# Hybrid decoder block on one core: heads 0 and 1 join the first seven-product column group, now 768 columns wide in six PSUM banks

## The chip, the cores and the metric

The kernel runs on one core of one Trainium2 chip. The metric is the device time of one execution in microseconds (us); the median of three runs of the kernel before is 1599.9 us. The engines are PE (TensorE, matmuls), ACT (ScalarE), DVE (VectorE), POOL (GpSimd) and SP, whose queue issues most transfers.

## The reference

The block normalizes `x` (1024 tokens by 2048), multiplies it by one wide input matrix, runs three groups of heads on the columns of the product, gates them, and adds an output projection:

```
h = rmsnorm(x, ln_g);  proj = h @ w_in          # 1024x2048 by 2048x7184
(g_u, g_v, g_z, d_q, d_k, d_v, d_z, d_a, d_b, c_q, c_z) = split(proj)
out_a = gmlp_spatial_gating(g_u, g_v, ...) * silu(g_z)
q, k, v = split(causal_conv_silu(concat(d_q, d_k, d_v), conv_w))   # 8 heads of 128 each
out_b = rmsnorm(gated_delta_rule(l2norm(q), l2norm(k), v, g, beta)) * silu(d_z)
out_c = softmax((c_q @ mk^T)) @ mv * silu(c_z)  # mk, mv from 256 memory rows
y = rmsnorm(x + concat(out_a, out_b, out_c) @ w_out)
```

Only the columns of q, k and v of the delta heads (group B), heads 0 to 3, and what feeds them are touched by the change.

## The kernel before, in words

**Products.** Every float32 operand is split into a rounded high part (ACT copies it to the float32r type) and a low part (DVE subtracts), by `split_to` (L445); a product of two blocks is then three matmuls, high by high, high by low, low by high (`triple`). A matmul has a 128 x 128 stationary block and 512 moving columns (tokens here).

**Stages.** First the keys and values of the memory rows are made (16 blocks of the contraction, `kvmark`), while `x`'s first 512 tokens are normalized, transposed on PE and split into the resident tiles `ahq`, `alq` (16 blocks of 128 contraction rows; `ahi[k]`, `alo[k]`). Then comes the stage that the change rewrites:

- Heads 0 and 1 have their q and k columns (four blocks of 128 columns) projected directly, for each half of the tokens: `project_first` (L889) for the first column block, `project` (L876) for the others, called from `conv` (L913). One column block and one token half is 16 contraction blocks times three matmuls. `project_first` runs its sixteen blocks twice with 256 tokens each, so that it can begin before the last 256 tokens are ready. After the first half of the tokens, `x`'s second half is normalized and transposed (`prep1`, L773), kept in plain form in tiles of the rings `ut`, `kT`, `qT`, `kd`, `ai`, `vs`, `gt`, and split once more into `ahq`, `alq` for the second half's projections. Banks: `main_bank` (L420) gives acc0 and acc1 to the projections in turn, `tpb` (L424) acc2 and acc3 to the transposes of `prep1` and to the decays.
- `decay_mm`, `decay_rows`, `decays` (L802 to L817) make the decay and beta columns of all heads, for each half.
- `left_sums` (L753) makes four sums and differences of the left factor's quarters and stores them to DRAM (`s_all`, in the profile `sa`); `whole` (L747) stores the plain left factor (`h0d`).
- Then the columns go two groups of 512 at a time through a scheme of seven products in place of eight: the left factor (tokens by contraction) is cut into 2 x 2, the two column groups and the two halves of the contraction make the right factor's 2 x 2, and `seven` (L1338) runs seven products of 512 tokens by 1024 contraction rows by 512 columns. `ORDER` is 2, 1, 6, 5, 3, 7, 4: products 2 and 1 make the first output quarter, product 1's sum stays in PSUM and 6, 7 and 4 accumulate on it. Four banks hold a product (`wide`, L1311), one for each block of 128 columns. For each product, right blocks are loaded from `w_in`, combined on DVE, and split; left blocks are loaded from `h0d`, `hTd` or `sa` and split. `blocks(5)` (L1510) does so with the q and k columns of heads 2 and 3 as one group (512 columns) and v of heads 0 to 3 as the other.

**Fronts.** `front` (L1174) does, for two heads and one token half, the convolution (`conv`), the transposes and small products of `qk` (L950), stores q, k, kd and ai for later (`late`), and feeds the 32 x 32 blocks to `inverse` (L1007). Fronts of heads 0 and 1 read their q and k from PSUM, those of the other heads from DRAM (`pd`). `backs` (L1495) later runs the recurrent scan of each pair of heads. After `blocks(5)` follow `blocks(0)` to `blocks(4)` with four banks each, and the output projection.

**Order.** Operations are not issued in program order: `Plan` records them all with a cost, a class (`rank`) and their dependencies, simulates the engines, and issues each engine's instructions in the simulated order. Main matmuls have class 9; whatever is ready with a lower class goes ahead of them. A tile that takes another tile's place (`heir`) waits for all users of the old one. All instructions carry the line of `issue` (L300) in the profile, so groups are told apart by tile.

Of the kernel before, what the change touches and what calls it, by code (L numbers as in the profile page):

```python
# [303 lines left out]
def kernel(  # L304
# [95 lines left out]
    for r in (wraw, whi, wlo):  # L400
        r.bufs = [b[:, i * HT : (i + 1) * HT] for b in r.bufs for i in range(2)]
    whi.bufs.append(C([P, HT], "whi4", F32R))
    wlo.bufs.append(C([P, HT], "wlo4", F32R))
# [14 lines left out]
    turn = {"acc": 0, "tp": 0, "dn": 0}  # L418

    def main_bank():  # L420
        turn["acc"] += 1
        return acc[turn["acc"] % 2]

    def tpb():  # L424
        turn["tp"] += 1
        return acc[2 + turn["tp"] % 2]
# [21 lines left out]

    def raw_piece(src, cls=4):
        raw = wraw()  # L450
        v = raw if src.ndim == 2 else raw.rearrange("p (k c) -> p k c", k=src.shape[1])
        with rank(cls):
            Q.dma_start(v, src)
        return raw

    def split_piece(raw):
        hi, lo = whi(), wlo()
        with rank(2):
            split_to(hi, lo, raw, V)
        return hi, lo  # L460

    marks = []
# [48 lines left out]
    def load_x(tt, tag, after=(None,) * 4):  # L511
        x_rows[tt] = row_tiles(tag)
        for c in range(4):
            with behind(after[c] or R.gate):
                Q.dma_start(x_rows[tt][c], x[tt * P : (tt + 1) * P, c * HT : (c + 1) * HT])
# [45 lines left out]
    def prep(tt, put, bank):  # L561

        xq = x_rows[tt]
        r = row_scale(xq)
        for q in range(NQ):
            V.scalar_tensor_tensor(xq[q], xq[q], r, gb[q], op0=ALU.mult, op1=ALU.mult)
            tp = bank()
            for k in range(4):
                PE.transpose(tp[:, k * P : (k + 1) * P], xq[q][:, k * P : (k + 1) * P], ident)
            put(q, tok(tp))  # L570

    def keep_rows(dst, q, tt, tp):
        t = ring["tn"]()
        S.copy(t, tp.rearrange("p t c -> p (t c)"))
        Q.dma_start(dst[4 * q : 4 * q + 4, :, tt * P : (tt + 1) * P].rearrange("k p n -> p k n"), tok(t))
# [24 lines left out]
    for k in range(KT):  # L600
# [49 lines left out]
        if k == 13:  # L650
            load_x(3, "qT", (kvmark[10], kvmark[11], kvmark[11], kvmark[12]))
            with rank(2):
                prep(2, put0(2), spare)
# [6 lines left out]
    for mt in range(2):  # L660
        t = [ring["ai"](F32R) for _ in range(2)]
        S.activation(t[0], va[mt], AF.Copy, scale=rm[mt])
        V.scalar_tensor_tensor(t[1], va[mt], rm[mt], t[0], op0=ALU.mult, op1=ALU.subtract)
        for i in range(2):
            Q.dma_start(
# [3 lines left out]
    with rank(2):  # L669
        prep(3, put0(3), spare)  # L670
    for h in range(NX):
        t = ring["vs"](F32R).rearrange("p (s m) -> p s m", s=2)
        split_to(t[:, 0], t[:, 1], kfs[h], V)
        Q.dma_start(kv_d[0, h], t.bitcast(F32))
# [5 lines left out]
    Q.dma_start(rows[0:96], conv_w.rearrange("k (c p) -> (k c) p", p=P))  # L680
    Q.dma_start(rows[96:100], gmlp_ln_g[0].rearrange("(c p) -> c p", p=P))
    Q.dma_start(rows[100:104], gmlp_ln_b[0].rearrange("(c p) -> c p", p=P))
    Q.dma_start(rows[104:105], dn_norm_g)
# [7 lines left out]
    pt = dnr()  # L691
    PE.transpose(pt[:, 0:105], rows[0:105], ident[0:105, 0:105])
    cw = C([P, 96], "cw")
    V.tensor_scalar(cw, pt[:, 0:96], 0.5, None, op0=ALU.mult)
    col2 = C([P, 9], "col2")
    V.tensor_copy(col2, pt[:, 96:105])

    abf = ring["E"]()[:, 0 : KT * 16].rearrange("p (k c) -> p k c", c=16)
    Q.dma_start(abf, w_in[:, C_AB : C_AB + 16].rearrange("(k p) c -> p k c", p=P))
    abw = C([P, KT * 32 + 96], "abw", F32R)  # L700
    R.users[abw.tensor.name] = []
    V.tensor_scalar(abw[:, KT * 32 :], ident[:, 0:96], 0.0, None, op0=ALU.mult)
    abv = abw[:, 0 : KT * 32].rearrange("p (k c) -> p k c", c=32)
    S.copy(abv[:, :, 0:16], abf)
    V.tensor_tensor(out=abv[:, :, 16:32], in0=abf, in1=abv[:, :, 0:16], op=ALU.subtract)

    halo = C([P, 3 * NH // 2, 3], "halo")
    G.memset(halo, 0.0)
# [22 lines left out]
    pairs = ((C_Q + HT, C_K + HT), (C_DZ + HT, C_DZ), (C_DV + HT, C_V), (C_U, C_Z), (C_CZ, C_CQ), (None, C_DV))  # L731
# [9 lines left out]
    def blk(w, k, c0):  # L741
        if c0 is None:
            both_ = w[k * P : (k + 1) * P, C_Q : C_Q + 2 * DW].rearrange("p (s c) -> p s c", c=DW)
            return both_[:, :, 2 * P : NJ * P]
# [7 lines left out]

    def left_sums(tt, q):  # L753

        def rows_of(d, q):
            return d[4 * q : 4 * q + 4, :, tt * P : (tt + 1) * P].rearrange("k p n -> p k n")

        a, b = spares(), spares()
        c, d = x_rows[NT + tt][q], x_rows[NT + tt][q + 2]
        Q.dma_start(tok(a), rows_of(h0_d, q))  # L760
        Q.dma_start(tok(b), rows_of(h0_d, q + 2))
# [3 lines left out]
        V.tensor_tensor(out=b, in0=b, in1=a, op=ALU.subtract)  # L765
        for i, t in enumerate((d, a, c, b)):
            Q.dma_start(rows_of(s_all[i], q), tok(t))
# [5 lines left out]
    def prep1(i):  # L773
# [6 lines left out]
        prep(NT + i, put, tpb)  # L780
# [21 lines left out]
    def decay_mm(a, k):  # L802
        wk = abw[:, k * 32 : k * 32 + P]
        mm(a, wk, ahi[k], k == 0, False)
        mm(a, wk, alo[k], False, k == KT - 1)

    def decay_rows(a, tt):

        with R.together():
            for q in range(NQ):  # L810
                for j in range(4):
                    k = 4 * q + j
                    PE.matmul(a[j * 32 : (j + 1) * 32, tt * P : (tt + 1) * P],
                              abw[:, k * 32 : (k + 1) * 32].bitcast(F32), tok(x_rows[NT + tt][q])[:, j],
                              start=q == 0, stop=q == NQ - 1)

    def decays(hf, a, bank):  # L817

        NU, M = NT * NH, P if hf else 32
        ab = ring["tn"]()[0:M]  # L820
        with rank(1):
# [7 lines left out]
        with rank(1):  # L829
# [41 lines left out]
    def w_parts(c0, kp):  # L871

        src = w_in[kp * KP * P : (kp + 1) * KP * P, c0 : c0 + P].rearrange("(k p) c -> p k c", p=P)
        return [tok(t) for t in split_piece(raw_piece(src))]

    def project(c0s, order=range(KT // KP)):  # L876

        banks = [main_bank() for _ in c0s]
        for kp in order:
            ws = [w_parts(c0, kp) for c0 in c0s]  # L880
            for kk in range(KP):
                k = kp * KP + kk
                for a, (hi, lo) in zip(banks, ws):
                    triple(a, (hi[:, kk], lo[:, kk]), ahl(k), kp == order[0] and kk == 0, kp == order[-1] and kk == KP - 1)
                if kk == 0:
                    marks.append(R.ops[-3])
        return banks

    def project_first(c0):  # L889

        a, ws = main_bank(), [w_parts(c0, kp) for kp in range(KT // KP)]
        for lo, hi in ((0, NT // 2), (NT // 2, NT)):
            for k in range(KT):
                w = [t[:, k % KP] for t in ws[k // KP]]
                triple(a[:, lo * P : hi * P], w, [t[:, lo:hi] for t in ahl(k)], k == 0, k == KT - 1)
        return a

    def next_job():
        if todo:
            with behind(marks[-1]):  # L900
                todo.pop(0)()

# [7 lines left out]
    def column(which, h):  # L910
        return (C_Q, C_K, C_DV)[which] + h * P

    def conv(which, h, hf, o, a=None):  # L913
# [3 lines left out]
        if which < 2 and h < 2:  # L917
            if a is None:
# [912 lines left out]
```

## Time and profile before

| what | value |
|---|---|
| three runs | 1599.76, 1599.9, 1601.36 us |
| profiled execution: span from the first to the last instruction | 1597.8 us |
| profiled execution's own time | not given apart from the three runs; the median lies 2.1 us above the span |
| DVE busy | 1314.9 us (82%) |
| ACT busy | 1040.0 us (65%) |
| moved by DMA | 428.93 MB, mean 268 GB/s |

The page shows the busy share of each engine over the span, the chain of work that ended last, and groups of like instructions with their mean duration and the idle time ahead of them. Matmuls overlap, so that the distance between the starts of two matmuls, and not the duration of one, is what each costs. In this trace the memory stage ends at about 62.5 us, the direct projections and `blocks(5)` fill the time until about 350 us, and the output projection takes the last 300 us.

### The profile page before, as it was taken

How to read it: one execution, taken by the hardware profiler on the slowest of the kernel's cores; microseconds unless marked ns; L12 is line 12 of the kernel's file. 1: busy time of each engine (PE TensorE's matmuls, PEld its weight loads, DVE VectorE, ACT ScalarE, POOL GpSimd, SP SyncE). 2: the span in 40 equal slices, each digit the busy share in tenths (PEclk: the TensorE clock that was granted, in tenths of full speed). 3: DMA queues.
4: the chain of work that ended last, by engine and by line, in shares of the span. 5: the costliest groups of instructions: out<-in, count | busy, mean ns of one | idle time of the engine just before them, and what ended most of it. 6: DMA issues, size and time to landing. Idle time of an engine off the chain costs nothing.

```text
span 1597.8 us, 26025 instructions
## 1 busy us (share of the span) xinstructions
PE 1582.5 (99%) x8580; PEld 1332.5 (83%) x8580; DVE 1314.9 (82%) x2157; ACT 1040.0 (65%) x2184; POOL 278.6 (17%) x456
## 2 busy tenths in 40 slices
PE   9999999999999999999999999999999999999997
PEld 8878888888888888888888888888888888888886
DVE  6879899869899999998988776867778788778776
ACT  7767648747755788976666667676566874344355
POOL 0101202211411412324342233032000000000001
PEclk9999999999999999999999999999999999999999
DMA  9987997897689868997789875788878879688746
GB/s 340 300 246 206 355 337 229 273 333 249 191 272 339 277 219 295 323 315 242 239 271 341 257 260 178 252 305 279 288 244 260 263 250 335 201 281 279 228 146 241
DMA packets 272744, 428.93 MB, mean 268 GB/s; under 512 B 30633, under 2 KB 97762, under 8 KB 272610
## 3 DMA queue, kind: packets, MB, share of 16 engines
q1 hardware_dynamic: 251138, 371.02, 70.9%
q0 software_dynamic: 20864, 55.20, 10.4%
q8 instruction: 67, 1.10, 0.3%
q10 hardware_dynamic: 608, 1.06, 0.2%
q14 instruction: 67, 0.55, 0.1%
HBM read 339.58 MB, written 87.06 MB: 267 GB/s over the span
## 4 chain that ended last, share of the span: by engine, by line
PE 94%; DMA 2%; ACT 1%; DVE 1%; issue 1%; SPq 0%; POOLq 0%; POOL 0%; ACTq 0%; DVEq 0%
PE acc L300 73%; PE dn L300 22%; DMA qT<-in_x_dram 0%; DMA h0d<-tn 0%; ACT whi L300 0%; DMA wraw<-in_w_in_dram 0%; DMA kvd<-vs 0%; DMA y<-h0d 0%; DMA wraw<-in_w_mem_kv_dram 0%; ACT jk L300 0%; SPq L300 0%; ACT tn L300 0%; DVE wlo L300 0%; ACT ahi L300 0%; DVE kT L300 0%
## 5 line engine op out<-in xcount | busy, mean ns | idle before, releaser
L300 PE MATMUL acc<-ahi,whi 128*128 128x512 f32 (+1 forms) x1488 | 513.4, 392 | 2.3 <-ACT ahi L300 1.1
L300 PE MATMUL acc<-ahi,wlo 128*128 128x512 f32 (+1 forms) x1040 | 404.8, 391 | 0.2 <-DVE wlo L300 0.2
L300 PEld LDWEIGHTS acc<-ahi,whi 128*128 128x128 f32 x1488 | 278.1, 188 | 57.0 <-ACT ahi L300 1.3
L300 PE MATMUL acc<-alo,whi 128*128 128x512 f32 (+1 forms) x592 | 229.2, 387 | 0.0
L300 PEld LDWEIGHTS acc<-ahi,wlo 128*128 128x128 f32 x1040 | 195.5, 188 | 37.2 <-DVE wlo L300 0.6
L300 ACT CAST ahi<-raws 128x1024 fp32r<-128x1024 f32 x148 | 155.4, 1050 | 64.0 <-PE acc L300 27.7
L300 PE MATMUL acc<-ahi,zh 128*128 128x512 f32 x448 | 176.5, 394 | 0.0
L300 PE MATMUL acc<-alo,zh 128*128 128x512 f32 x448 | 176.3, 394 | 0.0
L300 PE MATMUL acc<-ahi,zl 128*128 128x512 f32 x448 | 176.3, 394 | 0.0
L300 ACT CAST whi<-wraw 128x1024 fp32r<-128x1024 f32 (+1 forms) x116 | 108.0, 932 | 94.4 <-PE acc L300 75.6
L300 DVE TENSOR_TENSOR wlo<-wraw,whi 128x1024 fp32r<-128x1024 f32 (+1 forms) x116 | 124.2, 1073 | 38.0 <-ACT whi L300 34.4
L300 PEld LDWEIGHTS acc<-alo,whi 128*128 128x128 f32 x592 | 111.4, 188 | 20.8
L300 POOL TENSOR_TENSOR small<-small,mhalf 128x1 f32<-128x1 f32 x26 | 17.3, 672 | 525.0 <-DVE small L300 525.0
L300 DVE TENSOR_TENSOR alo<-raws,ahi 128x1024 fp32r<-128x1024 f32 x74 | 90.3, 1220 | 19.0 <-ACT ahi L300 18.4
L300 ACT CAST ahi<-y 128x1024 fp32r<-128x1024 f32 x74 | 77.7, 1049 | 40.3 <-PE dn L300 19.2
L300 DVE TENSOR_TENSOR alo<-y,ahi 128x1024 fp32r<-128x1024 f32 x74 | 90.3, 1220 | 16.1 <-ACT ahi L300 15.9
L300 DVE TENSOR_TENSOR ahi<-raws,ahi 128x1024 fp32r<-128x1024 f32 x74 | 90.4, 1222 | 15.1 <-ACT ahi L300 14.5
L300 PEld LDWEIGHTS acc<-alo,zh 128*128 128x128 f32 x448 | 84.2, 188 | 16.3
L300 PEld LDWEIGHTS acc<-ahi,zl 128*128 128x128 f32 x448 | 84.2, 188 | 16.1
L300 PEld LDWEIGHTS acc<-ahi,zh 128*128 128x128 f32 x448 | 84.2, 188 | 16.0
L300 PE MATMUL dn<-whi,ahi 128*128 128x512 f32 x224 | 77.1, 389 | 0.0
L300 PE MATMUL acc<-whi,ahi 128*128 128x512 f32 x216 | 74.9, 392 | 0.0
(464 smaller groups left out, 3451.4 us busy)
## 6 DMA issues: line engine op xcount, KB each, us to landing
wraw<-in_w_in_dram SPq DMA_DIRECT2D x224, 256.0 KB, 4.4
raws<-sa SPq DMA_DIRECT2D x128, 256.0 KB, 4.4
y<-in_w_in_dram SPq DMA_DIRECT2D x96, 256.0 KB, 4.1
y<-sa SPq DMA_DIRECT2D x64, 256.0 KB, 4.2
wraw<-in_w_out_dram SPq DMA_DIRECT2D x64, 256.0 KB, 4.4
raws<-h0d SPq DMA_DIRECT2D x62, 256.0 KB, 5.3
raws<-sd SPq DMA_DIRECT2D x44, 256.0 KB, 2.9
pd<-y SPq DMA_DIRECT2D x40, 256.0 KB, 5.2
```

What stands on the lines that cost most here:

```text
L300: o.fn(*o.args, **o.kw)
```

## The change

The direct projections go. The first pair of column groups becomes 768 wide: one group holds q and k of heads 0 to 2, the other q and k of head 3 and v of heads 0 to 3 (`FIRST_COLS`). A new function runs the seven products with six blocks of 128 columns each, in acc0 to acc3 and dn0, dn1; transposes, decays and fronts share dn2 and dn3 meanwhile. The order of the products is 2, 1, 6, 7, 4, 5, 3. Products 2 and 1 take the left factor from the resident tiles of the first token half, without a load or a split; the second half of the tokens is no longer split into the resident tiles. The first three contraction blocks of product 2 run with 256 tokens at a time.

```diff
-    first = project_first(column(0, 0))
...
-    first = project([column(0, 0), column(1, 0)], (1, 0, 2, 3))
...
-    blocks(5, half_heads, first_values)
...
+    wide6 = acc + dnr.bufs[0:2]
+    FIRST_COLS = (((C_Q, 3 * P), (C_K, 3 * P)), ((C_Q + 3 * P, P), (C_K + 3 * P, P), (C_DV, HT)))
...
+    def first_product(m, take):
+        def left(j, u):
+            if m in (1, 2):
+                k = j + NH * (m == 2)
+                return ahi[k], alo[k]
+            if u == 0:
+                lefts[:] = h_left(m, (j, j + 1))
+            return [x_[:, u * HT : (u + 1) * HT] for x_ in lefts]
...
+        if m == 2:
+            begin = 3
+            ws = [right_first(m, j) for j in range(begin)]
+            for ts in (slice(0, H0), slice(H0, NT)):
+                for j in range(begin):
+                    for t in range(6):
+                        cell(t, j, ws[j], left(j, j % 2), ts)
+        held = []
+        for j in range(begin, NH):
+            a, w = left(j, j % 2), right_first(m, j)
+            if j >= NH - 2:
+                held.append((j, w, a))
+            else:
+                for t in range(6):
+                    cell(t, j, w, a)
...
+        for t in range(6):
+            for h in held:
+                cell(t, *h)
+            take(t, wide6[t])
```

`cell` is one `triple`. The order of the stage is now:

```diff
+    for i in range(NT):
+        prep1(i); decay_rows(strips, i); left_sums(i, 0); left_sums(i, 1)
...
+    for k in (*range(NH, KT), *range(NH)):
+        decay_mm(dnr.bufs[2], k)
...
+    first_product(2, lambda t, a: c11.append((t, a)))
+    ywide = [heir(ahq[2], "y0", "ahi2"), heir(alq[3], "y1w", "alo3"), heir(ahq[3], "y2w", "ahi3")]
...
+    for t, a in c11:
+        keep(yu6[t], a)
...
+    first_product(1, c11_done)
...
+        fronts((0, 0), (1, 0))
+        fronts((2, 0))
...
+    first_product(6, lambda t, a: keep(yz6[t], a))
+    first_product(7, lambda t, a: keep(yu6[t], a))
+    first_product(4, c21_done)
+    first_product(5, closing(1, 1, yu6))
...
+    first_product(3, closing(0, 1, yz6))
...
+        fronts((0, 1), (1, 1))
+        fronts((2, 1))
+        fronts((3, 1), (3, 0))
```

(The first hunk is folded onto one line here.) `fronts` takes any list of heads and halves and reads q and k from DRAM always. The right blocks of product 1 stay in `kept1`, eight tiles of 768 columns (the tile of the spatial weights `wsbt`, a slot of `inv`, `kvraw` and the space of `alq[2]`), and serve product 6 by differences in place (`meet`). `left_sums` no longer loads the plain left factor from DRAM, it adds the resident high and low parts, and stores three of the four sums; the fourth is made when product 3 loads its left blocks (`last_sum`). The weights of the first products have three raw slots (two of `kvraw` and a slot of `inv` that the memory stage holds to its end). The stores of the memory keys and values, their splits, the loads of `x` and the constants get other ranks, and `prep` takes the last two token blocks in the order of quarters 2, 3, 0, 1. The spare fifth bufs of the weight rings become two plain tiles `et`. `blocks(0)` to `blocks(4)`, the scan and the output projection keep their form.

446 lines of the change are left out of this document (237 added, 209 removed).

## Prediction

> **What bounds the kernel now.** I read the head of the page, then the chain of waits, then the busy time by stretches. First the page's span, its busy line, and the chain that ended last by engine:
>
> ```profile
> span 1597.8 us, 26025 instructions
> PE 1582.5 (99%) x8580; PEld 1332.5 (83%) x8580; DVE 1314.9 (82%) x2157; ACT 1040.0 (65%) x2184; POOL 278.6 (17%) x456
> PE 94%; DMA 2%; ACT 1%; DVE 1%; issue 1%; SPq 0%; POOLq 0%; POOL 0%; ACTq 0%; DVEq 0%
> ```
>
> PE is 94% of the chain, and idle for 1597.8 - 1582.5 = 15.3 us. As matmuls overlap, "busy" alone proves little; but if PE is never idle, each matmul that goes is worth the distance between two starts. The stretches of the stage that changes (62.5 to about 350 us) and of what follows show where PE is idle (us of the stretch, then busy time and instructions of PE, PEld, DVE, ACT, POOL, granted clock, DMA share, GB/s):
>
> ```profile
> 62.50:100.00 37.50, 33.78 (x215) 28.95 (x214) 31.62 (x75) 27.64 (x71) 2.80 (x4) 1.00 0.92 265
> 100.00:165.00 65.00, 64.67 (x435) 54.44 (x434) 56.71 (x112) 47.19 (x122) 8.35 (x12) 1.00 0.75 218
> 165.00:229.00 64.00, 63.82 (x303) 52.89 (x302) 57.69 (x113) 35.55 (x70) 10.87 (x21) 1.00 1.07 348
> 229.00:300.00 71.00, 71.00 (x331) 59.25 (x330) 64.71 (x98) 51.53 (x114) 15.82 (x23) 1.00 0.78 249
> 350.00:430.00 80.00, 80.00 (x374) 66.81 (x373) 73.96 (x109) 56.88 (x119) 12.57 (x23) 1.00 0.72 237
> 430.00:500.00 70.00, 70.00 (x315) 58.05 (x314) 63.55 (x115) 34.25 (x51) 14.27 (x25) 1.00 0.86 277
> 510.00:590.00 80.00, 80.00 (x386) 67.11 (x385) 73.60 (x118) 62.31 (x139) 28.05 (x46) 1.00 0.80 265
> 590.00:670.00 80.00, 80.00 (x381) 67.00 (x380) 72.08 (x113) 70.21 (x145) 23.15 (x30) 1.00 0.88 294
> ```
>
> From 62.5 to 165 us PE waits 3.72 + 0.33 = 4.05 us, later hardly at all, even where DMA runs at 348 GB/s and DVE at over 90%. The clock is full throughout. So the stage is bound by the count of matmuls, plus a few starting waits. Those of 62.5 to 90 us by name (waiter, releaser, us, times, longest):
>
> ```profile
> PE acc L300 <- DVE kT L300: 1.2, 1, 1.2
> PE acc L300 <- ACT ahi L300: 1.1, 1, 1.1
> PE acc L300 <- ACT whi L300: 0.9, 2, 0.6
> PE acc L300 <- DVE abw L300: 0.5, 1, 0.5
> ```
>
> **The change: matmuls.** What one costs comes from undisturbed runs in the chain of waits (start, us, what) and, for 256 columns, from the first and last of 37 steps in the timeline:
>
> ```profile
> 330.33 50.81 PE acc L300 x224
> 1415.42 43.52 PE dn L300 x192
> 63.35 0.28 PE L300 MATMUL acc<-alo,whi 128*128 128x256 f32 x1
> 67.78 0.28 PE L300 MATMUL acc<-ahi,wlo 128*128 128x256 f32 x1
> ```
>
> 50.81 / 224 = 0.2268 us and 43.52 / 192 = 0.2267 us for 512 columns; 4.43 / 37 = 0.120 us for 256. Before: four column blocks x two halves x 16 x 3 = 384 direct products, of which 48 run as 96 with 256 columns, and `blocks(5)` has 7 products x 8 contraction blocks x 4 x 3 = 672. That is 1008 x 0.2268 + 96 x 0.120 = 240.1 us. After: 7 x 8 x 6 x 3 = 1008, of which product 2's first three contraction blocks (54) run as 108 halves: 954 x 0.2268 + 108 x 0.120 = 229.3 us. **The difference is -10.8 us**: the direct part had eight block products where seven do, 48 matmuls of 384. All of it lies on PE, which has no idle time to absorb it.
>
> [...]
>
> **The change: small work on PE.** The sixteen groups of four transposes of the second token half, the decay matmuls and the fronts' transposes stay, with new banks. A group of four costs, by these rows:
>
> ```profile
> 78.10 0.60 PE L300 MATMUL acc<-ident,ut 128*128 128x128 f32 x4
> 78.46 0.36 PE L300 MATMUL acc<-alo,whi 128*128 128x256 f32 x1
> 78.66 0.28 PE L300 MATMUL acc<-ahi,wlo 128*128 128x256 f32 x1
> ```
>
> 78.66 - 78.10 = 0.56, less 0.12 of the matmul between, 0.44 us. The number stays, so this term is 0; `decay_rows` in four bundles in place of one could add three such breaks at most, 0.3 us.
>
> **The change: waits at the start.** Two places are new. The first is the third weight block of product 2: its raw slot is held by the memory stage to its last matmul.
>
> ```profile
> 62.48 0.40 PE L300 MATMUL dn<-whi,inv 128*128 128x512 f32 x1
> 63.16 0.36 PE L300 MATMUL acc<-ahi,whi 128*128 128x256 f32 x1 [0.28 <-ACT whi L300]
> wraw<-in_w_in_dram SPq DMA_DIRECT2D x224, 256.0 KB, 4.4
> ```
>
> Issued at about 62.9, it lands 4.4 us later (median of a 256 KB load), and then must be split. The splits by shape are (shape, count, busy, mean ns):
>
> ```profile
> L300 ACT CAST whi<-wraw 128x512 fp32r<-128x512 f32 x31 | 19.1, 620 | 16.4 <-PE acc L300 13.9 <-DMA wraw<-in_w_in_dram 1.1 <-issue 1.1
> L300 ACT CAST whi<-wraw 128x1024 fp32r<-128x1024 f32 x14 | 14.7, 1049 | 11.4 <-PE acc L300 11.4
> L300 DVE TENSOR_TENSOR wlo<-wraw,whi 128x512 fp32r<-128x512 f32 x31 | 21.0, 686 | 5.9 <-ACT whi L300 5.4 <-DMA ut<-h0d 0.4
> L300 DVE TENSOR_TENSOR wlo<-wraw,whi 128x1024 fp32r<-128x1024 f32 x14 | 17.1, 1220 | 10.6 <-ACT whi L300 10.6
> ```
>
> 768 columns lie halfway: 0.83 us on ACT, 0.95 us on DVE, so the low part is there at about 62.9 + 4.4 + 1.8 = 69.1. PE by then has the first two blocks with 256 tokens, 36 x 0.120 = 4.3 us from 62.9, and two groups of transposes, 0.9: until 68.1. Estimate 1 us, bounds 0 and 3.2 (a landing half as slow again, 2.2 us).
>
> The second: product 1 overwrites the banks of product 2, which are copied first to the places of `ahq[2]`, `alq[3]` and `ahq[3]`; those wait for `decay_mm` of the upper contraction blocks, and that for dn2, which all of `prep1` and `decay_rows` use before. In the trace of before the last transposes and the decay rows end here:
>
> ```profile
> 111.15 0.60 PE L300 MATMUL acc<-ident,gt 128*128 128x128 f32 x4
> 111.68 1.08 PE L300 MATMUL acc<-ut,abw 128*32 128x128 f32 x32
> ...
> 114.76 0.62 PE L300 MATMUL acc<-gt,abw 128*32 128x128 f32 x16
> L300 PE MATMUL acc<-ahi,abw 128*128 128x512 f32 x16 | 6.5, 407 | 0.5 <-DVE abw L300 0.5
> ```
>
> Product 2's own PE time until there: 62.9 + 90 x 0.2268 + 108 x 0.120 (its whole and half matmuls: 33.4) + 20 transposing groups x 0.44 (8.8; four are still due from the first half) + decay rows 3.5 (111.68 to 115.2) + the wait above = 109.6. If the decay rows end as late as before, at 115.2, PE stands 5.6 us; the decay matmuls (32 x 0.2268 = 7.3 us) come after it either way. But `prep1` was late before for reasons that go: one of its two banks was held by `decay_mm` in between, and `vs` tiles that waited for memory stores of a low rank. Estimate 2 us, bounds 0 and 7.8 (2.2 us more, half a landing, for loads queued behind weight blocks).
>
> Of the waits of before, those for `abw` and `kT` (1.7) and for the last tokens' split (1.1) can go, and the first for `whi` shrinks. So 4.05 us go and about 1 + 2 + 1 (others of this kind) come: 0 net, bounds -4.05 and +7.5.
>
> **The change: work beside PE.** Costed at nothing, with these covers. The split of the second half into the resident tiles (sixteen copies on ACT and subtractions on DVE at 0.62 and 0.69 us) and the 32 small weight splits go; left loads for products 2 and 1 go. A contraction block of 768 columns lasts 18 x 0.2268 = 4.08 us on PE, and asks DVE for at most a difference (0.95), a weight split (0.95) and half a left split (0.61), 2.5 us; before it was up to 1.9 us for 2.72 us of PE. So DVE is better covered in the stage than before. DMA for a block: 393 KB of weights and 262 KB of left factor in 4.08 us, 160 GB/s, before 524 KB in 2.72 us, 193 GB/s; beside the 348 GB/s that the trace carried without PE waiting. Fetches are two or three instructions in place of one on SP's queue: fewer than four for 4.08 us of PE.
>
> Fronts move. Before, six of the sixteen (head, half) fronts lay ahead of 350 us (18 of 48 of the rows below); after, three. DVE then has three more for the stretches from 350 on:
>
> ```profile
> L300 DVE SCALAR_TENSOR_TENSOR qT<-xr,cw,qT 128x512 f32<-128x512 f32 x18 | 13.4, 746 | 0.2
> L300 DVE TENSOR_TENSOR inv<-qT,inv 128x512 fp32r<-128x512 f32 x6 | 4.1, 686 | 0.2 <-ACT inv L300 0.2
> L300 DVE TENSOR_TENSOR gt<-dn,E 128x256 f32<-128x256 f32 x12 | 5.0, 417 | 2.7 <-PE dn L300 1.5 <-ACT E L300 1.1
> ```
>
> One front: 6 x 0.75 + 5 x 0.69 (two for tanh, two for splits, one for the decay) + 4 x 0.42 = 9.6 us, three 29 us. In the four stretches above from 350 DVE is free 6.0 + 6.5 + 6.4 + 7.9 = 26.8 us. So the fronts will slide, by up to 29 us; weight splits have the better class and go first. The end of the scan has room for it:
>
> ```profile
> L300 PE MATMUL dn<-states,qT x112: 270/275/275, 758.8 to 1159.5; 128*128 128x128 f32 x112
> 1207.08 0.57 ACT L300 COPY kT<-acc 128x512 f32<-128x512 f32 x1
> ```
>
> The scan leaves its `kT` tiles at 1159.5 and the cross attention first writes them at 1207.1, 47.6 us later. Cost 0; if that cover were gone, every us beyond 47.6 less 10.8 would count.
>
> **The sum.** -10.8 + 0 (waits) + 0.0 to 0.3 (breaks): the span goes from 1597.8 to about 1587 us, and with the 2.1 us between span and median to **1589.1 us**, 0.7% less.
>
> **The rivals.**
> - *Product 1 stands.* The chain `prep1`, `decay_rows`, `decay_mm`, copy is later than product 2's end by 5 to 8 us. For it: in the trace of before it ended at 115.2 against 109.6 needed, and 0.92 of DMA was taken there. Against: what held it goes. 1592 to 1597. [...]
> - *DVE bounds the following groups.* The 29 us of fronts do not slide but stand ahead of weight splits in the planned order, and over a third of them (10.8 us) become waits of PE: about 1599, no change. For it: 26.8 us free for 29. Against: DVE was as full before (73.96 of 80), with no wait of PE.
> - *Slower: two banks are too few.* With acc0 to acc3 and dn0, dn1 held, the sixteen transposing groups and four decay rows alternate in dn2 and dn3, each after a copy by ACT; PE takes its instructions in order, so a late copy stops the products too. At the 1.24 us of the one such wait before (for `kT`), twenty make 24.8 us: 1589.1 + 24.8, some 1614 at worst, 1605 with thirteen; it is slower by over 0.2% from twelve waits on (10.8 + 3.2 us). Against: before, they also had two banks at a time, with one such wait in sixteen.
> - *A matmul is worth less than its row.* If part of the distance between starts is other work that stays, 48 matmuls give up the mean of all of PE's instructions, 1582.5 / 8580 = 0.184 us: 8.9 us, 1591. Against: the same 0.2268 in two places of the chain. [...]
>
> **How the numbers follow.** The forecast 0.66; product 1 stands 0.14; the price of a matmul 0.04; DVE 0.08; two banks 0.08. A difference below 0.2% (3.2 us) cannot be told from none here. Faster: 0.66 + 0.14 + 0.04 = 0.84, same 0.08, slower 0.08. The range goes from all starting waits gone (1589.1 - 4.1 = 1585) to their upper bound (1589.1 + 7.5 = 1597); it leaves out 0.16.
>
> **What would show it.** Right: PE has 276 to 279 us from 62.5 to the end of the stage instead of 287; 336 + 96 + 672 projecting matmuls become 954 + 108, 42 instructions fewer; waits of 3 to 5 us in all after 62.5, none after 165; later stages as long as before. Wrong: a wait of over 5 us at product 1 (on ACT's copies to `y`, or on `prep1`'s tiles), many waits on dn tiles, PE idle between 340 and 660 us with DVE as releaser, or a scan that ends after 1200 us.

## Result and profile after

The changed kernel takes 1613.64 us (median of 4 runs, 1613.28 to 1614.86), the kernel before in the same session 1599.83 us (4 runs, 1597.58 to 1601.36). The ratio is 1.0088 with a 95% interval of 1.0074 to 1.0103: slower by 13.8 us, where 10.8 us less was predicted. The profiled execution took 1613.38 us. The head of its page, with the chain that ended last by engine:

```profile
span 1611.4 us, 26264 instructions
PE 1581.3 (98%) x8538; PEld 1325.7 (82%) x8538; DVE 1310.2 (81%) x2209; ACT 1023.9 (64%) x2185; POOL 310.8 (19%) x499
PE 78%; DMA 9%; DVE 7%; ACT 2%; issue 2%; SPq 2%; POOL 0%; DVEq 0%; POOLq 0%; ACTq 0%
```

PE has the 42 instructions fewer that were counted. But it is idle for 1611.4 - 1581.3 = 30.1 us, where it was idle for 15.3, and its share of the chain fell from 94% to 78%: DMA, DVE and ACT now release it. The stretches show where (columns as in the prediction's table):

```profile
62.50:100.00 37.50, 31.21 (x259) 27.19 (x260) 31.01 (x65) 24.47 (x60) 5.11 (x7) 0.95 0.92 278
100.00:165.00 65.00, 64.11 (x354) 51.14 (x351) 49.45 (x120) 23.40 (x49) 1.38 (x3) 1.00 0.91 258
165.00:229.00 64.00, 59.11 (x255) 48.03 (x256) 55.76 (x99) 37.81 (x88) 7.52 (x14) 0.95 0.78 241
229.00:300.00 71.00, 71.00 (x339) 59.42 (x339) 55.51 (x115) 45.02 (x113) 19.41 (x32) 1.00 0.85 268
300.00:360.00 60.00, 57.36 (x274) 47.17 (x273) 54.20 (x98) 41.87 (x114) 22.03 (x33) 1.00 0.93 313
350.00:430.00 80.00, 80.00 (x378) 66.89 (x377) 74.09 (x118) 57.38 (x126) 28.88 (x46) 1.00 0.82 273
```

In the stage that changed PE is idle for 6.29 + 0.89 + 4.89 + 2.64 = 14.7 us, and in two of the stretches the granted clock is 0.95. The waits of PE from 60 to 360 us by name:

```profile
PE dn L300 <- ACT kT L300: 3.6, 1, 3.6
PE dn L300 <- DVE kT L300: 3.5, 2, 2.2
PE acc L300 <- DVE y L300: 3.2, 1, 3.2
PE dn L300 <- DVE alo L300: 1.6, 1, 1.6
PE acc L300 <- DVE xr L300: 1.4, 1, 1.4
PE dn L300 <- ACT jk L300: 1.3, 2, 1.0
```

With three of 0.2 to 0.3 us these are 15.3 us. The kernel before had 4.2 us in the same stretch, none of it ahead of a product in a dn bank. Here 10.7 us stand ahead of a dn bank; 0.2 us of them are for an accumulator of the wide product (dn0, dn1), 10.5 us for the small work in dn2 and dn3, in eight waits. The releaser's tiles tell two kinds apart: 6.5 us end with an instruction that empties the bank (`kT<-dn`, `alo<-dn`, `jk<-dn`), and 3.8 us with one that makes an operand (two of `kT<-tn,kT`, ahead of a head's transposes, and one of `sc`); 0.2 us are of neither kind. The kernel before has no wait of the first kind on a small bank there.

**Two of them followed to their start.** The longest, on ACT (start, us, what, and in brackets the idle time ahead of it and its releaser), and PE beside it:

```profile
86.73 0.25 ACT L300 COPY xr<-dn 128x128 f32<-128x128 f32 x1
91.23 0.63 ACT L300 ACTIVATE jk<-vs 128x512 bf16<-128x512 f32 x1 [4.25 <-DMA vs<-in_x_dram]
91.77 0.19 ACT L300 ACTIVATION_READ_ACCUMULATOR jk<-vs 128x1 f32 x1
91.86 1.05 ACT L300 COPY kT<-dn 128x512 f32<-128x512 f32 x2
```

```profile
88.46 0.40 PE L300 MATMUL dn<-ahi,inv 128*128 128x512 f32 x1
92.48 0.90 PE L300 MATMUL dn<-ident,qT 128*128 128x128 f32 x3 [3.62 <-ACT kT L300]
```

ACT took these in order: it is idle for the 4.25 us to 91.23 us, ahead of the square of a row tile that has not landed; the two copies that empty both small banks come behind it, at 91.86, though the transposes that they copy had ended by 87.7; PE's transposes need a bank and start at 92.48, and the next product of PE follows them, at 94.10. Three queues, each worked off in order here, turn a late load of 256 KB into 3.62 us of PE. The second long wait has the same form on DVE, where a subtraction waits for a weight block of product 6, and product 1's evacuating addition stands behind it:

```profile
162.36 0.68 DVE L300 TENSOR_TENSOR y<-acc,y 128x512 f32<-128x512 f32 x1
166.19 0.69 DVE L300 TENSOR_TENSOR y<-kT,y 128x512 f32<-128x512 f32 x1 [3.15 <-DMA kT<-in_w_in_dram]
166.80 0.68 DVE L300 TENSOR_TENSOR y<-acc,y 128x512 f32<-128x512 f32 x1
```

The granted clock (second last but one number) behind these two waits:

```profile
88.00:92.30 4.30, 0.86 (x4) 0.37 (x2) 3.20 (x6) 1.07 (x3) 0.86 (x1) 0.95 1.00 315
92.30:95.30 3.00, 2.82 (x11) 2.63 (x12) 0.00 (x0) 2.85 (x9) 0.00 (x0) 0.50 1.03 356
95.30:100.00 4.70, 4.70 (x53) 3.66 (x52) 4.22 (x9) 2.34 (x6) 0.86 (x1) 1.00 0.82 241
164.00:167.20 3.20, 0.36 (x2) 0.00 (x0) 1.01 (x2) 0.00 (x0) 0.00 (x0) 0.96 1.03 362
167.20:174.00 6.80, 6.30 (x14) 4.24 (x15) 5.28 (x10) 0.00 (x0) 0.00 (x0) 0.52 0.91 287
174.00:180.00 6.00, 6.00 (x28) 4.96 (x27) 2.40 (x4) 1.30 (x3) 0.00 (x0) 1.00 0.98 311
```

PE works on at half clock for 3.0 and for 6.8 us, which costs up to 3.0 x 0.50 + 6.8 x 0.48 = 4.8 us that no view of waits shows.

**The whole account.** For each pair of matmuls that follow each other I took the distance of their starts less a price for the first (0.227 us for 512 columns and 0.120 for 256, as measured; 0.060 for 128 and 64 and 0.030 for 32, which are estimates from the 0.120, the same for both kernels; for 128 the median distance is 0.109 in both traces), and summed what is left over; I call it PE's loss. It holds waits, half clock and breaks together. The times at full clock sum to 1513.0 us before and 1502.2 after: the 10.8 us of the prediction are there, and the distance is unchanged (43.52 / 192 = 0.2267 us):

```profile
1472.14 43.52 PE acc L300 x192
```

The loss by stretches (us; the stage ends near 360, the scan runs from about 750 to 1170):

| kernel | 60 to 160 | 160 to 360 | 360 to 740 | 740 to 1200 | whole span |
|---|---|---|---|---|---|
| before | 7.5 | 3.9 | 4.5 | 44.5 | 74.8 |
| after | 13.7 | 16.1 | 8.9 | 47.0 | 99.2 |

24.4 more, less 10.8, is the 13.6 us by which the span grew. 18.4 of the 24.4 us arise in the stage itself: 11.1 are the longer waits named above (15.3 less 4.2), up to 4.8 the half clock, the rest breaks too short to be named.

### The profile page after: what moved, and what is told of

It is laid out like the page before. It is cut to its first block, busy times and chain, and to the rows that moved or that the text cites. A ratio compares the mean times of both kernels' runs of the same rounds, so it can differ in the third digit from the quotient of the medians.

```text
span 1611.4 us, 26264 instructions
## 1 busy us (share of the span) xinstructions
PE 1581.3 (98%) x8538; PEld 1325.7 (82%) x8538; DVE 1310.2 (81%) x2209; ACT 1023.9 (64%) x2185; POOL 310.8 (19%) x499
## 3 DMA queue, kind: packets, MB, share of 16 engines
q0 software_dynamic: 22016, 55.21, 10.2%
## 4 chain that ended last, share of the span: by engine, by line
PE 78%; DMA 9%; DVE 7%; ACT 2%; issue 2%; SPq 2%; POOL 0%; DVEq 0%; POOLq 0%; ACTq 0%
PE acc L300 55%; PE dn L300 23%; SPq L300 2%; DVE wlo L300 1%; DMA wraw<-in_w_in_dram 1%; DMA vs<-in_x_dram 1%; DVE qT L300 1%; DMA y<-in_w_in_dram 1%; DMA raws<-h0d 1%; DVE alo L300 1%; DMA qT<-in_w_in_dram 1%; DVE kT L300 1%; DMA kT<-in_w_in_dram 1%; DMA gd<-y2w 0%; ACT whi L300 0%
## 5 line engine op out<-in xcount | busy, mean ns | idle before, releaser
L300 PE MATMUL acc<-ahi,whi 128*128 128x512 f32 (+1 forms) x1328 | 455.5, 393 | 1.4 <-ACT y L300 1.4
L300 PE MATMUL acc<-ahi,wlo 128*128 128x512 f32 (+1 forms) x904 | 354.3, 393 | 0.0
L300 PEld LDWEIGHTS acc<-ahi,whi 128*128 128x128 f32 x1328 | 248.5, 188 | 50.3 <-ACT y L300 1.8
L300 PEld LDWEIGHTS acc<-ahi,wlo 128*128 128x128 f32 x904 | 169.9, 188 | 32.9
L300 PE MATMUL acc<-alo,whi 128*128 128x512 f32 (+1 forms) x480 | 187.5, 391 | 0.0
L300 DVE TENSOR_TENSOR wlo<-wraw,whi 128x1024 fp32r<-128x1024 f32 (+1 forms) x80 | 94.3, 1179 | 22.1 <-ACT whi L300 19.9
L300 ACT CAST whi<-wraw 128x1024 fp32r<-128x1024 f32 (+1 forms) x80 | 81.4, 1017 | 47.9 <-PE acc L300 32.9
L300 PEld LDWEIGHTS acc<-alo,whi 128*128 128x128 f32 x480 | 90.7, 189 | 17.0
L300 DVE TENSOR_TENSOR alo<-y,ahi 128x1024 fp32r<-128x1024 f32 x65 | 79.7, 1226 | 17.1 <-ACT ahi L300 16.9
L300 PEld LDWEIGHTS acc<-alo,zh 128*128 128x128 f32 x424 | 79.9, 188 | 15.2
L300 ACT CAST ahi<-y 128x1024 fp32r<-128x1024 f32 x65 | 68.3, 1050 | 37.9 <-PE acc L300 19.5
```

Source lines behind the costliest of these rows:

```text
L300: o.fn(*o.args, **o.kw)
```

## Experiments

Theory Q: TensorE stands because an ACT or DVE instruction that waits for a transfer is queued ahead of an evacuation; the two waits above with their half clock are the cause. Rival B: with six banks held, two are too few for the small work beside the products. Rival D: DVE has no room. A fourth, L, came later: the planner's order is one of many, and a new order costs or saves by chance. "Stage" is the loss from 60 to 360 us: 11.4 before, 29.8 after. Medians stand beside about 1599.8 us for the kernel before in each session.

**The two waits taken away by an order.** In `first_product(1)`'s evacuations and the subtractions of product 6, and in `prep1`:

```diff
+        r = fresh(0, 1, j)
+        with behind(c11_adds[-1] if j >= 3 else None):
+            meet(0, kept1[j], r)          # e1, e3
...
+            with behind(copied[1] if i == 3 else None):
+                prep1(i)                  # e2, e3
```

> Edit: from the fourth on, the differences that turn the kept right blocks into product 6's wait for product 1's last evacuating add, so that they stand behind the six adds in DVE's queue. Theory Q (a DVE or ACT instruction that waits for a transfer at the head of its queue holds the PSUM copies behind it, PE stands over 3 us and then runs a few us at half clock): the wait of 3.2 us at product 6 and the half clock of 6.8 us behind it (3.4 us lost) go, about 1607 us, one half-clock stretch left in the middle. Rival D (DVE is too full, the wait only moves): 1612 to 1614, the same sum of waits elsewhere. Rival B (two banks too few): says nothing of this wait, as it is on an acc bank; the rest of the loss stays in waits on dn banks.

> Edit: the whole preparation of the last 128 tokens of the second half waits for the last copy of the second 128, so that ACT's squares on a row tile that has not landed stand behind the copies of transposes. Theory Q: the wait of 3.6 us at about 88 us and the half clock of 3.4 us behind it (1.7 us lost) go, about 1608.5 us, the other half-clock stretch stays. Rival B (two banks too few for the transposes): the transposes go on waiting for their copies, at other places, sum of the waits on dn tiles before 120 us as large as in the changed kernel (7 us), 1612 to 1614.

> Both edits. Theory Q: the two gains add, 12 us, about 1601.5 us, no half-clock stretch between the start and the end, and the clock's mean near 0.999. Rival B or D: less than 5 us of it, 1609 or more, with the waits in other places.

Measured: 1623.11 us (ratio 1.0148, 1.0133 to 1.0163), 1615.39 (1.0099, 1.0079 to 1.0119) and 1620.8 (1.0137, 1.0120 to 1.0153). All three missed the times that Q gave; of the rivals' times only e3's (1609 us or more) was met. The gate of e1 also kept the raw slots of product 6, so that its weights were fetched late; it tells nothing of its question, but it makes one wait long:

```profile
PE acc L300 <- ACT zh L300: 15.2, 1, 15.2
```

In e2 the wait at 88 us did go, yet the stage lost 30.3 us: others came ahead of the small work (two for a bank that `sc` empties, 3.8 us, one for a bank that `kd` empties, 2.8, and two for the operand `kT`, 3.9). So taking that one wait away gained nothing: others took its place.

**Two banks in the kernel before.**

```diff
-        return acc[2 + turn["tp"] % 2]
+        return dnr.bufs[2 + turn["tp"] % 2]          # tpb: rows, decays (e4, e14)
...
-        qt, kt = to_tokens((q, scan_banks[0]), (k, scan_banks[1]))
+        qt, kt = to_tokens(*zip((q, k), (work(), work()) if h < 2 else scan_banks))   # heads 0, 1 (e4, e13)
```

> The kernel before, with its transposes of the second half, its decays and the fronts of heads 0 and 1 confined to dn2 and dn3, as in the changed kernel (acc2, acc3, dn0 and dn1 stand idle meanwhile). Theory Q: the banks are no cost of their own, within 2 us of 1599.8. Rival B: the two banks bring the waits of the changed kernel, at least 5 us: 1605 or more, with new waits on dn tiles before 230 us.

> The kernel before with the query and key transposes of heads 0 and 1 in the two banks in which the rest of a head's small products goes, where they had two banks of their own; the rows keep theirs. Rival B (banks): the heads' work waits for its own evacuations, 160 to 360 us lose 5 to 12 us more than the 3.9 us of the kernel before, 1605 to 1613 us. Rival L (chance of a new order): as the two new orders of the kernel before, 1603 to 1609 us, with the loss after 700 us and not in 160 to 360 us.

> The kernel before with the transposes of the second half's rows and the sums of the decays in the two banks of the heads' small products, where they had two banks of their own. Rival B (banks): 1610 to 1625 us, most of the 32 us that both edits together cost, since the rows' transposes and the chain of the decays are what the trace of that run showed waiting. Rival L: 1603 to 1609 us.

Measured: both together 1632.44 us (1.0211, 1.0193 to 1.0228), the heads alone 1603.69 (1.0023, 1.0014 to 1.0033), the rows alone 1619.92 (1.0134, 1.0117 to 1.0151); stages of 43.2, 13.2 and 29.6 us. The times of e4 and e14 are those that B gave; e13's is not, but L's. The same work in two banks loses up to 32 us, but not evenly: the heads' transposes cost 2 us more in the stage, while with the rows and decays in them most is one wait, for the chain of the decays:

```profile
PE dn L300 <- DVE sc L300: 12.1, 1, 12.1
```

The granted clock is 0.55 and 0.53 in the 15 us that follow 186 us. This wait is not for a bank: the product needs `sc` itself, and DVE is busy for 9.57 of the 10 us from 186 to 196 us, with the decays' short steps in turn with sums of the left factor. Only in e4 are waits of PE seen that end when a small bank is emptied (7.2 us); in e13 and e14 there are none. So what two banks cost in this kernel hangs on what stands at the head of PE's queue, and that the banks themselves cost it is shown by e4 alone.

**Less work beside the products.** The three heads that run in the stage moved behind it (e7), then one head (e16), then the mixing matrices (e15); e15 and e16 on the order of e5, below:

```diff
-    with rank(5.5):
-        fronts((0, 0), (1, 0))
-        fronts((2, 0))
...
     with rank(2.6):
+        with behind(chunk_ends[-1]):
+            fronts((0, 0), (1, 0))        # e7
+            fronts((2, 0))                # e7, e16
...
+    with rank(7), behind(chunk_ends[-1]):
+        token_mix()                       # e15
```

> The changed kernel with the three fronts that run beside the first pair of column groups (heads 0, 1 and 2 of the first half) moved behind it, where four banks are free for them again. The work is the same. Rival B (two banks too few for the work beside the products): the waits at 203, 302, 324 and 344 us go (2.4, 1.5, 0.5 and 1.1 us, with the excess of 160 to 360 us down by 6 to 8 us from 16.1), and little comes after 380 us: 1605 to 1609 us. Theory D (VectorE has no room after the stage either, the three fronts bring 29 us more of it there): what goes before 360 us comes back after it, 1611 to 1618, with waits for VectorE between 380 and 700 us. Theory Q alone (the two long waits are the cause): those stay, 1608 to 1614.

> The changed kernel with transfers counted on 1.5 us later (1601.7 us) and the mixing matrices of the first part (four transposes, eight small products in the two banks, whose first product waited up to 3.1 us in three orders) moved behind the first pair of column groups. Rival B: less work in the two banks gives 1 to 4 us: 1597 to 1601 us. Rival L: a new draw, 1602 to 1615 us.

> The changed kernel with transfers counted on 1.5 us later (1601.7 us) and one of the three heads of the stage (head 2) moved behind it. Rival B: 160 to 360 us lose 3 to 5 us less than the 10.8 us of that run, and a third of the work moved fits in the room behind (three heads did not: 1665 us): 1597 to 1602 us. Theory D (VectorE and the scan have no room behind the stage): the scan ends late, 1610 to 1625 us.

Measured: 1665.39 us (1.0415, 1.0399 to 1.0430), 1634.77 (1.0220, 1.0201 to 1.0240) and 1643.48 (1.0278, 1.0261 to 1.0294). None of the three times lies in a range that was given. In the stage B was right: 160 to 360 us lose 1.3 us instead of 16.1 in e7, and 7.9 and 7.7 instead of 10.8 in e15 and e16. PE of e7 there:

```profile
165.00:229.00 64.00, 64.00 (x282) 52.65 (x281) 44.13 (x76) 27.99 (x50) 0.00 (x0) 1.00 0.68 205
229.00:300.00 71.00, 71.00 (x319) 58.79 (x318) 46.49 (x82) 29.91 (x52) 1.05 (x2) 1.00 0.79 241
```

No idle time. All of it and much more comes back later, since the heads are the start of a chain: their blocks are inverted on DVE, and the scan waits for the inverses. First and last start of an inverse's step, and of a scan's step, in after, then in e5, and then in e16:

```profile
L300 DVE TENSOR_TENSOR et<-inv,inv x62: 178/353/422, 455.5 to 821.9; 128x31 f32<-128x31 f32 x4, 128x60 f32<-128x60 f32 x4, 128x87 f32<-128x87 f32 x4, 128x112 f32<-128x112 f32 x4
L300 PE MATMUL dn<-states,qT x112: 270/275/275, 774.5 to 1172.7; 128*128 128x128 f32 x112
```

```profile
L300 DVE TENSOR_TENSOR et<-inv,inv x62: 182/356/424, 452.3 to 802.0; 128x31 f32<-128x31 f32 x4, 128x60 f32<-128x60 f32 x4, 128x87 f32<-128x87 f32 x4, 128x112 f32<-128x112 f32 x4
L300 PE MATMUL dn<-states,qT x112: 270/275/275, 758.8 to 1193.1; 128*128 128x128 f32 x112
```

```profile
L300 DVE TENSOR_TENSOR et<-inv,inv x62: 182/360/877, 547.8 to 905.0; 128x31 f32<-128x31 f32 x4, 128x60 f32<-128x60 f32 x4, 128x87 f32<-128x87 f32 x4, 128x112 f32<-128x112 f32 x4
L300 PE MATMUL dn<-states,qT x112: 270/275/421, 850.6 to 1245.1; 128*128 128x128 f32 x112
```

One head, 9.6 us of DVE by the prediction's rows, starts the inverses 95 us later than in e5, on whose order e16 stands, and ends the scan 52 us later. PE then waits for the scan's steps and loses 48 us after 1200, where e5 and after lose 4. So the scan's room was there only for a chain that starts on time. e15 shows that more than the heads' own work can delay it: it moves no head, yet the sixth of its sixteen convolutions starts at 400 us where e5's starts at 329, its inverses start at 519.9 us, and its scan ends at 1236.6. Why the mixing matrices hold up that convolution was not followed up.

**Margins in the plan.** The planner counts on a transfer landing 2.9 us after its bytes have moved, and puts what PE takes from another engine 0.6 us later than that engine's end. Each edit is a number:

```diff
-    SLACK = 600.0
-    DMA_FIXED = 2900.0
+    DMA_FIXED = 4400.0     # e5; e8: the kernel before; e10, e11: 3000 in after, before; e12: 3900; e17: 5000
+    SLACK = 1800.0         # e6; e18: 800, with DMA_FIXED 4100
...
+            R.extra = 4500.0 if xq is x_rows.get(NT + 3) else 0.0    # e9: added to that instruction's due time
+            S.activation(jk, xq[c], AF.Square, accum_out=s[:, c : c + 1])
...
+        R.extra = 3500.0
+        meet(0, kept1[j], r)
```

> The changed kernel with one constant of the planner raised, so that it counts on each transfer 1.5 us later (2.9 us to 4.4 us fixed) and lets other work go in front of what waits for one. Theory Q (TensorE stands because an ACT or DVE instruction that waits for a transfer is queued ahead of the evacuation that TensorE needs; two such waits of 3.8 and 3.3 us, and 1.7 and 3.4 us of half clock behind them): both waits go, 1602 to 1606 us. Rival B (with six banks taken, two banks are too few for all the work beside the products; each chain waits for its own evacuations, whatever the planner counts on): within 4 us of 1613.6. Rival L (luck of the order: any new order shuffles the waits, with a spread of some 10 us either way): anything between 1605 and 1625, with the long waits at other places.

> The changed kernel with a margin at the two places alone where an instruction that waited for a transfer stood in front of TensorE's evacuations: the planner counts on the squares of the last rows 4.5 us later, and on the subtractions of product 6 3.5 us later; every other price is as in the changed kernel, though the order behind these places follows from it. Theory Q (these two waits and the half clock behind them are most of the loss): 1601 to 1605 us. Rival L (any new order draws new waits; the 1601.7 us of the run with all transfers counted on later was a lucky draw): 1608 to 1622 us, with waits elsewhere. Rival B (two banks are too few, some 1 to 2 us at each place): 1607 to 1612 us.

> The changed kernel with the planner's margin for what another engine gives to TensorE raised from 0.6 to 1.8 us, so that transposes and small products are put 1.2 us later into TensorE's queue, behind more matmuls of the products. Theory M (the evacuations come later on the chip than in the plan, so that TensorE reaches the small work too early): waits on the two small banks shrink by more than half between 60 and 360 us, 1600 to 1606 us. Rival B (two banks are too few): each turn of a bank lasts 1.2 us longer, and with some 100 turns in the stage the last products wait for the small work or it runs on past the stage: 1612 to 1620. Theory Q (waits of ACT and DVE for transfers): the two long waits stay or move little, 1610 to 1616.

> Control: the kernel before with the same constant of the planner raised (each transfer counted on 1.5 us later). Theory Q says that the kernel before has no such waits to lose: 1597 to 1602 us. Rival L (luck of the order) says that the kernel before stands on one good order among many, so that a new order of the same work costs 5 to 15 us: 1605 to 1615 us.

> The changed kernel with the planner's fixed time of a transfer at 3.0 us where it was 2.9 us: a change that means nothing, but after which thousands of instructions stand elsewhere in their queues. Theory Q, with its two waits bound to the numbers of the plan: one or both may stay, 1605 to 1616 us. Rival L: a draw anywhere between 1600 and 1622 us. It measures how much of a difference between two orders of the same work is chance.

> The kernel before with the same meaningless nudge (3.0 us for 2.9 us). Rival L, that the kernel before stands on a lucky order: 1604 to 1612 us. If its order is not special: 1598 to 1603 us.

> The changed kernel with the fixed time of a transfer at 3.9 us (2.9 us in the changed kernel, 4.4 us in the run that gave 1601.7 us). Theory Q: the margin helps by degrees, the squares' wait of 4.3 us and the subtraction's of 3.2 us shrink to 3 us and less, so that the half clock behind them goes: 1601 to 1608 us. Rival L: a draw anywhere between 1600 and 1622 us.

> The changed kernel with every transfer counted on 2.1 us later (5.0 us fixed, 2.9 us in the changed kernel). Theory Q with its margin (waits for transfers in the queues of ACT and DVE are what the changed order loses to): 60 to 360 us lose 16 to 22 us as with 1.0 and 1.5 us (21.8 and 21.9) and not the 26 to 31 us of the orders without the margin; 1597 to 1604 us if the scan comes no later than in the changed kernel. Rival L (chance): 60 to 360 us lose 25 to 31 us, 1608 to 1616 us.

> The changed kernel with each transfer counted on 1.2 us later (4.1 us fixed) and the margin of what another engine gives to TensorE at 0.8 us (0.6 us). Theory Q with its margin: 60 to 360 us lose 16 to 22 us, 1598 to 1605 us. Rival B (banks): the longer margin at TensorE makes each turn of a small bank 0.2 us longer, no gain over the run with transfers alone, 60 to 360 us lose some 22 us, 1602 to 1606 us. Rival L: 60 to 360 us lose 25 to 31 us, 1608 to 1616 us.

Measured, with the loss in the stage and behind it (us):

| order | median | ratio, interval | stage | 360 to 1200 |
|---|---|---|---|---|
| before (2.9) | 1599.83 | | 11.4 | 49.0 |
| e11, before, 3.0 | 1605.27 | 1.0040, 1.0023 to 1.0056 | 12.2 | 53.3 |
| e8, before, 4.4 | 1608.33 | 1.0057, 1.0042 to 1.0072 | 14.0 | 54.9 |
| after (2.9) | 1613.64 | 1.0088, 1.0074 to 1.0103 | 29.8 | 55.9 |
| e10, after, 3.0 | 1611.67 | 1.0075, 1.0052 to 1.0098 | 31.0 | 52.3 |
| e9, after, at two places | 1609.81 | 1.0063, 1.0048 to 1.0078 | 25.8 | 55.0 |
| e12, after, 3.9 | 1612.44 | 1.0082, 1.0065 to 1.0099 | 21.8 | 59.8 |
| e18, after, 4.1 and 0.8 | 1605.95 | 1.0035, 1.0022 to 1.0048 | 27.0 | 48.9 |
| e5, after, 4.4 | 1601.69 | 1.0009, 1.0000 to 1.0018 | 21.9 | 49.6 |
| e17, after, 5.0 | 1602.05 | 1.0016, 1.0007 to 1.0024 | 20.8 | 50.0 |
| e6, after, 2.9 and 1.8 | 1676.51 | 1.0476, 1.0457 to 1.0495 | 31.3 | 44.6 |

Four things follow. First, chance has a size: 0.1 us in one constant moves the kernel before up by 5.8 us (its session had 1599.44) and the changed one down by 2.0. The order of before, with no wait of PE from 360 to 1250 us, is a good one that its neighbours are not. Second, a margin for transfers goes with less loss in the changed kernel's stage and not in that of the kernel before: three orders with it alone (e12, e5, e17) lose 21 to 22 us there, those with 2.9 or 3.0 us and no margin at a single place (after, e10, e6) 30 to 31. The gain has the form that Q gives it: in e5 and e17 the named waits fall from 15.3 to 10.0 and 9.8 us, and the stretches at half clock in the stage from 10.2 us to 3.4. e12 gives this back by one wait of 4.8 us in the scan and 13.7 us at half clock behind it; e18 missed its 16 to 22. Third, Q's two waits alone are not it: in e9 both are gone, and this one comes, for the operand `kT`, while DVE works without a gap from 189.4 to 199.9 us. It is neither for a bank nor behind a transfer; there D holds for ten microseconds:

```profile
PE dn L301 <- DVE kT L301: 3.7, 1, 3.7
```

Fourth, even the best orders keep 7 to 10 us of loss more than the orders of before. The longest waits of e17 from 60 to 360 us:

```profile
PE dn L300 <- ACT jk L300: 3.1, 1, 3.1
PE dn L300 <- DVE alo L300: 1.9, 1, 1.9
PE dn L300 <- ACT ut L300: 1.7, 1, 1.7
PE dn L300 <- DVE kT L300: 1.3, 2, 0.9
```

9.3 of its 9.8 us stand ahead of a dn bank; in e5 8.1 of 10.0, in the nudged kernel before 0.9 of 4.0. Not all of that is the two small banks: 0.4 and 0.7 us are for accumulators in dn0 and dn1, and others are for an operand. Waits of over 0.15 us on small work that end when its bank is emptied, by an instruction that makes no operand of it, are 5.5 us in e17 and 5.7 in e5, and 1.6 to 6.5 us in each of the seven orders after, e9, e10, e12, e18, e5 and e17; the three orders of the kernel before (2.9, 3.0 and 4.4) have 0, 0 and 0.4. Part of the difference between the kernels is thus the banks, whatever the order. e6 failed in another place: with 1.2 us more at each step of the scan on PE, the scan runs to 1278 us, and 74 us are lost after 1200:

```profile
PE dn L300 <- ACT vs L300: 15.7, 10, 3.9
PE dn L300 <- DVE steps L300: 9.6, 6, 5.8
```

As to the times that were foretold: e17 met Q's, and e5 lies 0.3 us below them; e8, e11 and e12 met only L's; e9 met B's and L's, e10 Q's and L's; e18 has B's time with L's loss in the stage; e6 met none.

No order of the change that was tried beats the kernel before as it is. With the same constant in both kernels the change costs 13.8 us at 2.9, 6.4 at 3.0, and gains 6.6 at 4.4 (e5 against e8), so its sign hangs on the order.

## Why the prediction was wrong

- *The matmuls*: right to 0.1 us. 1513.0 - 1502.2 = 10.8, 42 instructions fewer, 0.2267 us each.
- *Waits at the start*: about right in sum, not by place. To 88 us PE waits 1.4 (`xr`) and 1.6 us (`alo`), and the third weight block causes none; then come the 3.62 us for `prep1`'s banks; PE is idle for 6.29 + 0.89 = 7.18 us to 165 us, 3.1 more than before, within the bounds of -4.05 and 7.5. Product 1 does not stand: 0.89 us idle from 100 to 165 us. That rival fell.
- *"Work beside PE. Costed at nothing, with these covers"*: **this step failed.** The covers were sums, so much DVE time and so much DMA for a block of 4.08 us, and they hold: from 100 to 300 us DVE is less busy than before (49.45 for 56.71, 55.76 for 57.69, 55.51 for 64.71 us). What was not asked is in which order each engine takes its work, and where that order is held up. The forecast's "none after 165" became 8.2 us of waits up to 360 us and 4.3 behind, and up to 4.8 us are lost at half clock in the stage. In PE's loss, the term that was put at nothing is 12.2 us from 160 to 360 us (16.1 less 3.9) and 6.9 from 360 to 1200 (55.9 less 49.0).
- *"Slower: two banks are too few"*, given 0.08: its 1605 to 1614 us hold the measured time, though not by its sum: it priced thirteen to twenty waits of 1.24 us, and the profile shows eight on the small work, of 0.2 to 3.6 us, with half clock beside them. It was set aside with "before, they also had two banks at a time, with one such wait in sixteen". That counted the rows alone: before, rows had acc2 and acc3, a head's transposes dn0 and dn1, its other products dn2 and dn3. The mechanism was narrower than the truth too: of the 18.4 us, 8 to 9 go with a margin for transfers (e5, e12, e17); 9 to 10.5 stay in these too, a good half of it in waits for one of the two banks to be emptied (5.7 us in e5, 5.5 in e17).
- *DVE bounds the following groups*: as it was put, no. From 350 to 590 us PE has no idle time. But "cost 0" for moving heads was right only for the three that the change moves: the scan ended at 1172.7 instead of 1159.5, and one more head moved costs 42 us (e16 against e5). In single places DVE did hold PE up, as for 3.7 us in e9.
- *Part of the loss is order.* Mean over the changed kernel's seven orders of like kind (after, e9, e10, e12, e18, e5, e17): 1608.2 us; over three of before (before, e11, e8): 1604.5. By that the change costs some 4 us where 10.8 were to be gained, but single orders lie up to 7 us from their mean, so that seven and three of them do not show that it costs anything on the whole. The two kernels of the study differ by 13.8. Sums of durations could not have told one order to 0.3%.

What stays open: how much the stage would lose with four small banks. Six accumulators of 512 columns and four small ones do not fit the eight that the kernel has, so this wasn't tried; that the last 10 us are in good part the banks rests on where the waits stand and what ends them, on e7, e15 and e16, and on e4 in the other kernel, and no run shows how much of it a better order of the same six and two banks would save. It is also open why the constant 4.1 with the longer margin (e18) lost 27 us, and why e15 delayed the scan.

## What to carry to other kernels

A saving on the bounding engine is worth its price only if that engine's queue stays fed (here 10.8 us of matmuls went and 24.4 us of loss came): count the buffers that each kind of small work turns over in, before and after, and follow one buffer's release through the queues of the engines that give it back, for a load that is late ahead of it. Price a wait of TensorE with the half clock that the trace shows behind it (here up to 1.5 and 3.3 us behind waits of 3.62 and 3.18). When an order written by a planner changes, nudge a constant that means nothing, in both kernels, and compare several orders, before a difference of half a per cent is put down to the change.

## What was not expected of the hardware

The clock. In before's trace it was full throughout the stage (1.00 in every stretch). Here it was halved in and behind the waits of 3.62 and 3.18 us (0.50 and 0.52), of 15.2 us in e1 (0.68 from 163 to 179 us) and of 12.1 in e14 (0.55 from 186 to 196 us), and in e10 behind a wait of 1.9 us, for 3.3 us:

```profile
203.00:207.00 4.00, 2.13 (x12) 1.67 (x13) 3.59 (x8) 4.00 (x10) 0.68 (x2) 0.99 0.71 185
207.00:210.30 3.30, 3.30 (x9) 2.60 (x8) 3.30 (x7) 2.71 (x11) 0.00 (x0) 0.50 0.67 220
```

A wait of 3.1 us in e17, at 320 us, was followed by none (1.00 from 319 to 332 us). The clock records of after give three stretches: 3.41 us from 91.86 us and 6.83 us from 166.95 us, both of which start inside the wait and go on behind it, and one from 1607.38 us that the end of the trace cuts off. Their starts lie on a grid that the waits do not set: the second and the third start 22 and 444 times 3.413 us after the first. In e6's trace those behind the first start 17, 38, 93, 348, 351, 360, 368, 370, 395 and 486 times 3.413 us after it. By this grid the two cases differ: in e10 the whole 1.87 us of idle PE lie between two of its points (203.54 and 206.95 us), while in e17 a point at 321.77 us cuts the 3.06 us into 1.25 and 1.81. That this is why was not shown, nor how much idle time halves the clock: it was halved behind 1.87 us idle beside transposes, and not behind 1.81 us.
